# Weight loads issued by ScalarE on their own queue in a two-layer hybrid recurrent decoder

## The chip, the core and the metric

The kernel runs on one core of a Trainium2 chip. A core has a matmul engine (TensorE, PE in the profile, with its weight loads as PEld), three engines for elementwise work (VectorE or DVE, ScalarE or ACT, GpSimd or POOL) and SyncE (SP), which computes nothing and here issues transfers. Each engine takes its own instructions in order; they meet through semaphores. The metric is the device time of one execution in microseconds. Lower is better.

## The reference

One inference step of two layers, in float32, for a prompt of 1024 tokens and for 8 sample sequences of one token each, with the same weights; 1032 token columns in all, model width 1024.

```python
# layer 0
xn = rms(x); proj = xn @ w_in0                      # 1024 x 4632, 24 of the columns are gates
conv_act = silu(causal_conv(conv_in))               # 2560 channels, width 4
y  = group_rms((ssd_scan(...) + d * xs) * silu(z))  # Mamba-2, 16 heads, chunks of 128
hm = (group_rms(mlstm_scan(q, k, v, ...)) + skip * xm) * sigmoid(o)   # 4 heads
x += concat([y, hm]) @ w_out0
x += (silu(rms(x) @ w_gate) * (rms(x) @ w_up)) @ w_down               # hidden 2816
# layer 1
xx = shift(rms(x)) - rms(x)                         # six mixtures xr, xw, xk, xv, xa, xg
r, k, v = xr @ wr, xk @ wk, xv @ wv                 # and low-rank w, a, g
S_t = S_{t-1} diag(w_t) + (S_{t-1} (-kk_t)) (kk_t a_t)^T + v_t k_t^T  # RWKV-7, 16 heads
x += ((group_norm(S_t r_t) + bonus) * g) @ wo
x += swiglu(rms(x))
y = rms(x)
```

All new recurrent states are returned too.

## The kernel before

Activations lie transposed: 128 features on the partitions, token columns along the free dimension, so a matrix product is a loop over tiles of 128 output features, each the sum over 8 tiles of 128 inputs. Float32 products are made of three passes. Every operand is cast to a coarser float32 form (`hi`) and the remainder (`lo`) is kept; `mm3` sums lo times hi, hi times lo and hi times hi.

Weights are therefore read, and then prepared, one output tile at a time, in `wload`: a transfer of 128 x 1024 numbers (512 KB) into a tile `raw`, of which the pool `wraw` has two buffers; then, for each half, ScalarE casts to `whi` (`S.copy`, L175) and VectorE subtracts to get `wlo` (`tt`, through the helper's L145). The pool `whl` has four buffers of 512 columns for `whi` and four for `wlo`. A raw buffer is free for the next weight as soon as VectorE has read its last half. Three places load weights: `wload` (L169), `wdown` in the feed-forward, which reads a row tile of the down projection (L968), and `lora2` in the RWKV projections (L1084). The names in the profile follow the tiles: `raw_g`, `raw_u`, `rawd` (feed-forward gate, up, down), `raw_rw` (RWKV r, k, v), `raw_o` (output gate and output projection of layer 0), `raw_wo`, `raw_in`, `raw_z`, `raw_gate`, and `rawl2w`, `rawl2a`.

All transfers are issued by SyncE, through `dma = SY.dma_start`: these weight loads, the inputs, and the many intermediate tensors that go through scratch memory (`scr_...`), among them the small blocks that the RWKV scan exchanges (`scr_ablk`, `X`, `scr_tblk`, `obd`, `scr_toff`, `tbd`, `vbd`) and the projections' results (`rst`, stored by L1119 from a ring of two buffers).

Work runs in this order, in time of the profiled execution. Until about 850 us: the norm, the input projection with the convolutions, the SSD and mLSTM chunks, the gates' tiles and the output projection for the first half of the tokens. From 850 to 1230: the feed-forward of layer 0 for the first half, with the second half's output projection between. From 1230 to 2000: RWKV projections of the first half, then the scan of the first half (`rwkv_scan`, generators `rw_pre`, `rw_inv`, `rw_front`, `rw_fin`, `rw_ln`) woven into the feed-forward of the second half. From 2000 to 3000: projections of the second half, its scan, the decode steps and the first feed-forward of layer 1. From 3000 on: the last output projection and feed-forward, with no scan beside it.

The order within each engine is not written by hand. The program's text gives each instruction a priority (its place, shifted ahead by `ahead()` for a few), the framework plans the instructions against a model of their times, and places all semaphore waits. Each engine's list, the issues on it included, then runs in that fixed order. So when the issuing engine of a transfer changes, the plan is made anew.

Of the kernel before, what the change touches and what calls it, by code (L numbers as in the profile page):

```python
# [90 lines left out]
def _body(tc, nc, I, O, top):  # L91
    def pool(stack, name, bufs=1, **kw):
        if kw.get("space") is not DRAM:
            kw["reuse_waits"] = "tile"
        return stack.enter_context(tc.tile_pool(name=name, bufs=bufs, **kw))
# [15 lines left out]

    V, S, G, PE, SY = nc.vector, nc.scalar, nc.gpsimd, nc.tensor, nc.sync
    dma = SY.dma_start

    consts = cp.tile([128, NLATE], F32, name="consts")
    dma(out=consts, in_=I["consts"][:, 0:NLATE])
# [27 lines left out]
    def tt(out, a, b, op=ALU.mult, e=None):  # L144
        (e or V).tensor_tensor(out=out, in0=a, in1=b, op=op)  # L145

    def stt(out, a, s, b, op0=ALU.mult, op1=ALU.mult, e=None):
        (e or V).scalar_tensor_tensor(out=out, in0=a, scalar=s, in1=b, op0=op0, op1=op1)  # L148
# [4 lines left out]
    def act(out, a, f, **kw):  # L153
        S.activation(out, a, f, **kw)  # L154
# [11 lines left out]
    def wload(src, name, n=1024, step=128, e=None, th=TA_, p=128):  # L166

        raw = th.wraw.tile([128, 1024], F32, name="raw_" + name, tag="raw")
        dma(out=raw[0:p, 0:n], in_=src)  # L169
        out = []  # L170
        for c0 in range(0, n, 512):
            m = min(512, n - c0)
            hi = th.whl.tile([128, 512], F32R, name=f"whi_{name}{c0}", tag="whi")
            lo = th.whl.tile([128, 512], F32R, name=f"wlo_{name}{c0}", tag="wlo")
            S.copy(hi[0:p, 0:m], raw[0:p, c0:c0 + m])  # L175
            tt(lo[0:p, 0:m], raw[0:p, c0:c0 + m], hi[0:p, 0:m], ALU.subtract, e)
            for q in range(0, m, step):
                out.append((hi[0:p, q:q + step], lo[0:p, q:q + step]))
        return out
# [44 lines left out]
    def ahead():  # L224

        return tc.high_priority(offset=AHEAD)

    def norm_split(src, gname, tp, hl, blocks, base, bank=dbank):
        def emit(k, n0, n, x, g, rs):
            t = tp.tile([128, blocks[-1][1]], F32, name="n_t", tag="nq", bufs=2)  # L230
            stt(t[:, :n], x, g, rs)
            c = slice(n0 - base, n0 - base + n)
            split(t[:, :n], hl[k][0][:, c], hl[k][1][:, c])
        norm(src, gname, tp, emit, blocks, bank)
# [610 lines left out]
    def hl_ring(name, w):  # L845
        return [[H_.hl.tile([128, 520], F32R, name=f"{name}{q}{k}", tag="h" + q)[:, 0:w] for q in "hl"]
                for k in range(8)]
# [77 lines left out]
    def wide(name):  # L925
        return H_.nt.tile([128, 520], F32, name=name, tag="nt", bufs=2)

    def ffn(layer, hf, xs, hook=None, bank=dbank, start=None, ap=None, wide_=lambda f: True):
        base, W = HALF[hf]
        blocks, dblk = HBLK[hf], DBLK[hf]  # L930
        with ExitStack() as st:
            tp = H_.nt
            defer = ap is not None
            ap = ap or pool(st, f"ffna{layer}{hf}", GRP + 1)
            hl = hl_ring(f"f{layer}{hf}", W)
            with ahead():
                norm_split(lambda k, n0, n: xs[k][:, n0 - base:n0 - base + n], f"g_ffn{layer}", tp, hl, blocks, base, bank)
            if start:
                start()

            def up(f, part=False):
                nm = f"{layer}{hf}_{f}"
                wg = wload(I["wgu"][layer, f, 0], "g" + nm)
                wu = wload(I["wgu"][layer, f, 1], "u" + nm)
                ah = ap.tile([128, 520], F32R, name="ah" + nm, tag="ah")
                al = ap.tile([128, 520], F32R, name="al" + nm, tag="al")
                sg = wide("sg" + nm)

                def evg(n0, n, ps):
                    s = sg[:, n0 - base:n0 - base + n]  # L950
                    act(s, ps, AF.Tanh, scale=0.5)
                    stt(s, s, 1.0, ps, ALU.add, ALU.mult)

                def evu(n0, n, ps):
                    c = slice(n0 - base, n0 - base + n)
                    stt(sg[:, c], sg[:, c], 0.5, ps)
                    split(sg[:, c], ah[:, c], al[:, c])
                def tiles(bl):
                    dense_tile(wg, hl, "g" + nm, evg, blocks=bl, base=base)
                    dense_tile(wu, hl, "u" + nm, evu, blocks=bl, base=base)  # L960
                if part:
                    return (ah, al), tiles
                tiles(dblk if f and wide_(f) else blocks)
                return ah, al

            def wdown(f):
                raw = TA_.wraw.tile([128, 1024], F32, name=f"rawd{layer}{hf}{f}", tag="raw")
                dma(out=raw, in_=I["wdn"][layer, f])  # L968
                hi = ap.tile([128, 1024], F32R, name=f"dhi{layer}{hf}{f}", tag="dhi", bufs=GRP)
                lo = ap.tile([128, 1024], F32R, name=f"dlo{layer}{hf}{f}", tag="dlo", bufs=GRP)  # L970
                S.copy(hi, raw)  # L971
                tt(lo[:, 0:512], raw[:, 0:512], hi[:, 0:512], ALU.subtract)
                tt(lo[:, 512:], raw[:, 512:], hi[:, 512:], ALU.subtract)
                return hi, lo

            def down(f, acts, wds, bls=None):
                ev = resid(xs, base)
                for bl in bls or [dblk if wide_(f) else blocks]:
                    for m in range(8):
                        dense_tile([(w[0][:, m * 128:m * 128 + 128], w[1][:, m * 128:m * 128 + 128]) for w in wds],  # L980
                                   acts, f"d{layer}{hf}{f}_{m}", ev(m), blocks=bl, base=base)

            acts = {}
            split_ = hf == 1 and not defer
            for f in range(NFF - split_):
                acts[f] = up(f)
                if hook:
                    hook(f)
                if f % GRP == 0 and f:
                    g = range(f - GRP, f)  # L990
                    down(f, [acts[i] for i in g], wds)
                if f % GRP == GRP - 1:
                    wds = [wdown(i) for i in range(f - GRP + 1, f + 1)]
            if split_:

                acts[NFF - 1], tiles = up(NFF - 1, True)
                hook(NFF - 1)
                wds = [wdown(i) for i in range(NFF - GRP, NFF)]
                for q in blocks:
                    tiles([q])  # L1000
                    down(NFF, [acts[i] for i in range(NFF - GRP, NFF)], wds, [[q]])
            last = lambda bls: down(NFF, [acts[i] for i in range(NFF - GRP, NFF)], wds, bls)
            if defer:
                return lambda: last([[q] for q in blocks])
            if split_:
                return
            last([[q] for q in blocks])
# [13 lines left out]
    def rwkv_proj(hf, xs, xe, hook=lambda c, j: None, vt=None):  # L1021
        base, W = HALF[hf]
        blocks, dblk = HBLK[hf], DBLK[hf]
        with ExitStack() as st:
# [51 lines left out]
            def lora2(i, nm, bias, dst):  # L1076

                w = []

                def tile_(j):  # L1080
                    if j % 4 == 0:

                        raw = TA_.wraw.tile([128, 1024], F32, name=f"rawl2{nm}{hf}{j}", tag="raw")
                        dma(out=raw[:, 0:512], in_=I["wl2"][i, :, j * 128:j * 128 + 512])  # L1084
                        w[:] = [TA_.whl.tile([128, 512], F32R, name=f"l2{nm}{hf}{j}", tag="whi")]
                        S.copy(w[0], raw[:, 0:512])
                        tt(w[0][64:128], raw[64:128, 0:512], w[0][64:128], ALU.subtract)
                    o = j % 4 * 128
                    t = wide("l2t")
                    for n0, n in dblk:  # L1090
                        ps = dbank("l2ps")
                        c = slice(n0 - base, n0 - base + n)
                        PE.matmul(out=ps[:, 0:n], lhsT=w[0][:, o:o + 128], rhs=LH[i][0][:, c], start=True, stop=False)
                        PE.matmul(out=ps[:, 0:n], lhsT=w[0][:, o:o + 128], rhs=LH[i][1][:, c], start=False, stop=True)
                        act(t[:, c], ps[:, 0:n], AF.Tanh, bias=hw0[:, bias + j:bias + j + 1], scale=0.5)
                    dma(out=dst[:, j, base:base + W], in_=t[:, 0:W])
                return tile_
# [768 lines left out]
```

## Time and profile before

| | |
|---|---|
| median of 3 runs | 3487.57 us (3483.46 to 3492.62) |
| profiled execution | 3490.3 us, its span 3488.5 us |
| mean granted TensorE clock | 0.971 |
| TensorE busy | 3233.9 us, 93% |
| VectorE / ScalarE / GpSimd busy | 2329.8 / 1656.6 / 1228.5 us |
| DMA | 458.26 MB in 399135 packets, 43.6% of 16 engines' time on one hardware queue (q1) |

The span goes from the first to the last instruction. Busy shares are averages over stages with different limits, so a stage is read by itself: the rows of stages give start and end, length, and then the busy time and count of PE, PEld, DVE, ACT and POOL, the granted clock, the DMA share and GB/s. The chain is followed back from the last instruction through whatever released each step. A row of the waits says who waited, for whom, the total in us, how many times and the longest. SPq is SyncE's queue; a row of its timeline gives the start and the time that the issue itself took. Rows of one line's instructions give minimum, median and maximum in ns. In rows of groups stand the busy total and mean ns, then the idle time ahead.

### The profile page before, as it was taken

The page shows a single profiled execution, that of the slowest core. Times are in us where ns is not written, and L with a number is a line of the kernel's source. Part 1 is how long each engine was busy: PE and PEld are TensorE (multiplying, and loading weights), DVE is VectorE, ACT ScalarE, POOL GpSimd, SP SyncE. Part 2 cuts the span into 40 slices and gives each one's busy share as a digit, 9 for nine tenths or more (in the row PEclk, how much of TensorE's full clock was granted, in tenths as well). Part 3 has the DMA queues.
Part 4 walks back from the last instruction along what each step waited for, and adds up shares of the span by engine and source line. Part 5 has one row for each costly group of instructions (what it writes and reads, how often), then busy time and mean ns, then how long its engine had stood idle before and what let it go on. Part 6 is the DMA issues. An engine that isn't in the chain of part 4 may idle for free.

```text
span 3488.5 us, 61294 instructions
## 1 busy us (share of the span) xinstructions
PE 3233.9 (93%) x22615; PEld 2990.8 (86%) x22615; DVE 2329.8 (67%) x4315; ACT 1656.6 (47%) x3705; POOL 1228.5 (35%) x1586
## 2 busy tenths in 40 slices
PE   6999978998999999989999978988999899999998
PEld 6998877877778887779999968987888889999998
DVE  8866534566765477676776686667777775575555
ACT  5444344534243245655455565665555554452223
POOL 3334254121200002255645576237767873000000
PEclk9999998999999999999999989999999999999999
DMA  3456586663663343543333323462433333333232
GB/s 118 128 185 201 178 220 178 191 192 124 222 202 109 97 145 110 187 149 98 103 103 102 94 81 122 139 208 74 116 102 103 99 89 116 120 97 99 87 101 67
DMA packets 399135, 458.26 MB, mean 131 GB/s; under 512 B 154756, under 2 KB 295524, under 8 KB 398708
## 3 DMA queue, kind: packets, MB, share of 16 engines
q1 hardware_dynamic: 398836, 454.34, 43.6%
q8 instruction: 179, 2.93, 0.4%
q14 instruction: 120, 0.98, 0.1%
HBM read 352.10 MB, written 102.07 MB: 130 GB/s over the span
## 4 chain that ended last, share of the span: by engine, by line
PE 43%; DVE 13%; POOL 10%; DMA 8%; ACT 5%; issue 4%; SPq 1%; DVEq 0%; ACTq 0%; POOLq 0%
PE ps_g L186 9%; PE ps_d L186 9%; PE ps_u L186 9%; POOL X L145 4%; POOL t L145 4%; PE ps_rw L186 4%; PE ps_out L186 2%; ACT L154 2%; PE ps_o L186 2%; PE ps_wo L186 1%; DVE lp L148 1%; DMA phm<-scr_hmt 1%; DMA raw_rw<-in_wrw 1%; PE M L1403 1%; POOL y L145 1%
## 5 line engine op out<-in xcount | busy, mean ns | idle before, releaser
L186 PE MATMUL ps_d<-al,dhi 128*128 128x260 f32 (+2 forms) x1248 | 386.8, 310 | 20.3 <-DVE xa L145 5.0
L186 PE MATMUL ps_d<-ah,dlo 128*128 128x260 f32 (+2 forms) x1248 | 373.2, 299 | 0.0
L186 PE MATMUL ps_d<-ah,dhi 128*128 128x260 f32 (+2 forms) x1248 | 372.9, 299 | 0.0
L145 POOL TENSOR_TENSOR X<-X,t 32x30 f32<-32x30 f32 (+14 forms) x480 | 307.0, 640 | 32.6
L145 POOL TENSOR_TENSOR t<-X 32x30 f32<-32x30 f32 (+14 forms) x480 | 294.2, 613 | 30.9
L186 PEld LDWEIGHTS ps_d<-al,dhi 128*128 128x128 f32 x1248 | 237.2, 190 | 40.9 <-DVE xa L145 10.5
L186 PEld LDWEIGHTS ps_d<-ah,dlo 128*128 128x128 f32 x1248 | 237.4, 190 | 7.5
L186 PEld LDWEIGHTS ps_d<-ah,dhi 128*128 128x128 f32 x1248 | 236.9, 190 | 7.6 <-issue 0.2
L145 DVE TENSOR_TENSOR wlo_g<-raw_g,whi_g 128x512 fp32r<-128x512 f32 (+1 forms) x192 | 144.5, 755 | 106.1 <-ACT whi_g L175 104.2
L971 ACT CAST dhi<-rawd 128x1024 fp32r<-128x1024 f32 x88 | 88.4, 1046 | 216.6 <-PE ps_d L186 208.9
L154 ACT ACT_TABLE_LOAD x140 | 179.6, 1283 | 8.0 <-DVE ss L145 5.6
L175 ACT CAST whi_g<-raw_g 128x512 fp32r<-128x512 f32 (+1 forms) x192 | 113.9, 599 | 143.0 <-DMA raw_g<-in_wgu 83.3
L145 DVE TENSOR_TENSOR wlo_u<-raw_u,whi_u 128x512 fp32r<-128x512 f32 x176 | 133.9, 761 | 69.1 <-ACT whi_u L175 68.1
L175 ACT CAST whi_u<-raw_u 128x512 fp32r<-128x512 f32 x176 | 107.9, 619 | 134.7 <-PE ps_u L186 100.9
L186 PE MATMUL ps_in<-xnl,whi_in 128*128 128x344 f32 x480 | 155.5, 324 | 1.5 <-ACT ext L289 1.5
L186 PE MATMUL ps_in<-xnh,wlo_in 128*128 128x344 f32 x480 | 155.8, 325 | 0.0
L186 PE MATMUL ps_in<-xnh,whi_in 128*128 128x344 f32 x480 | 154.8, 322 | 0.0
L145 DVE TENSOR_TENSOR dlo<-rawd,dhi 128x512 fp32r<-128x512 f32 x176 | 124.4, 759 | 15.2 <-ACT dhi L971 15.1
L145 POOL TENSOR_TENSOR xx<-xa 128x512 f32<-128x512 f32 x8 | 9.7, 1242 | 346.5 <-PE ps_out L186 346.5
L157 ACT CAST ah<-sg 128x260 fp32r<-128x260 f32 (+2 forms) x155 | 67.5, 435 | 132.0 <-DVE sg L148 130.0
L145 DVE TENSOR_TENSOR wlo_rw<-raw_rw,whi_rw 128x512 fp32r<-128x512 f32 x96 | 72.1, 758 | 80.4 <-ACT whi_rw L175 76.8
L145 POOL TENSOR_TENSOR Bb<-Bc,consts 128x256 f32<-128x256 f32 x64 | 50.8, 793 | 210.3 <-PE M L1403 138.3
(959 smaller groups left out, 11934.7 us busy)
## 6 DMA issues: line engine op xcount, KB each, us to landing
raw_g<-in_wgu SPq DMA_DIRECT2D x88, 512.0 KB
raw_u<-in_wgu SPq DMA_DIRECT2D x88, 512.0 KB
rawd<-in_wdn SPq DMA_DIRECT2D x88, 512.0 KB
raw_rw<-in_wrw SPq DMA_DIRECT2D x48, 512.0 KB
raw_o<-in_wout SPq DMA_DIRECT2D x32, 512.0 KB
raw_in<-in_win SPq DMA_DIRECT2D x20, 512.0 KB
D<-scr_acr SPq DMA_DIRECT2D x16, 512.0 KB
Cs<-in_mc SPq DMA_DIRECT2D x16, 512.0 KB
```

Source lines behind the costliest of these rows:

```text
L145: (e or V).tensor_tensor(out=out, in0=a, in1=b, op=op)
L148: (e or V).scalar_tensor_tensor(out=out, in0=a, scalar=s, in1=b, op0=op0, op1=op1)
L154: S.activation(out, a, f, **kw)
L157: S.copy(hi, src)
L175: S.copy(hi[0:p, 0:m], raw[0:p, c0:c0 + m])
L186: PE.matmul(out=ps, lhsT=w[a], rhs=x[b], start=i == 0, stop=i == n - 1)
L971: S.copy(hi, raw)
L1403: PE.matmul(out=b[:, o + q * 128:o + q * 128 + 128], lhsT=lhs(q), rhs=rhs(q), start=True, stop=True)
```

## The change

A second name, `wdma`, is bound to ScalarE's `dma_start`, and the three places that load weights use it. All other transfers stay on SyncE. Buffers, sizes, casts and the number of transfers stay as they are.

```diff
     V, S, G, PE, SY = nc.vector, nc.scalar, nc.gpsimd, nc.tensor, nc.sync
     dma = SY.dma_start
+    wdma = S.dma_start
...
     def wload(src, name, n=1024, step=128, e=None, th=TA_, p=128):
         raw = th.wraw.tile([128, 1024], F32, name="raw_" + name, tag="raw")
-        dma(out=raw[0:p, 0:n], in_=src)
+        wdma(out=raw[0:p, 0:n], in_=src)
...
             def wdown(f):
                 raw = TA_.wraw.tile([128, 1024], F32, name=f"rawd{layer}{hf}{f}", tag="raw")
-                dma(out=raw, in_=I["wdn"][layer, f])
+                wdma(out=raw, in_=I["wdn"][layer, f])
...
                         raw = TA_.wraw.tile([128, 1024], F32, name=f"rawl2{nm}{hf}{j}", tag="raw")
-                        dma(out=raw[:, 0:512], in_=I["wl2"][i, :, j * 128:j * 128 + 512])
+                        wdma(out=raw[:, 0:512], in_=I["wl2"][i, :, j * 128:j * 128 + 512])
```

## The prediction, made before the change was run

> **What bounds the kernel now.** I read the page first, then the busy time by stage, then the waits of the DMA queue, then single stretches.
>
> ```profile
> span 3488.5 us, 61294 instructions
> PE 3233.9 (93%) x22615; PEld 2990.8 (86%) x22615; DVE 2329.8 (67%) x4315; ACT 1656.6 (47%) x3705; POOL 1228.5 (35%) x1586
> PE 43%; DVE 13%; POOL 10%; DMA 8%; ACT 5%; issue 4%; SPq 1%; DVEq 0%; ACTq 0%; POOLq 0%
> ```
> ```profile
> 0.00:850.00 850.00, 770.73 (x4561) 700.12 (x4562) 534.79 (x863) 389.11 (x928) 271.17 (x238) 0.96 0.57 170
> 850.00:1230.00 380.00, 372.13 (x1825) 298.36 (x1824) 230.87 (x385) 123.99 (x196) 29.25 (x24) 0.99 0.49 160
> 1230.00:2000.00 770.00, 734.75 (x5247) 678.95 (x5245) 547.17 (x1027) 407.44 (x877) 333.04 (x465) 0.99 0.42 123
> 2000.00:3000.00 1000.00, 886.65 (x7109) 847.57 (x7108) 723.86 (x1405) 566.15 (x1385) 595.04 (x860) 0.95 0.40 113
> 3000.00:3110.00 110.00, 107.79 (x879) 105.58 (x878) 75.65 (x174) 56.18 (x110) 0.00 (x0) 1.00 0.29 92
> 3110.00:3488.00 378.00, 361.83 (x3006) 360.27 (x3004) 217.47 (x464) 113.75 (x210) 0.00 (x0) 0.98 0.30 94
> ```
>
> TensorE (first number after the length) is the bound: 93% busy, 255 us idle in all. The feed-forward stretches (850 to 1230, 3000 to 3488) leave it idle 8, 2 and 16 us; nothing that moves DMA issues can matter there. The idle time sits in 0 to 850 (79 us), 1230 to 2000 (35 us) and above all 2000 to 3000 (113 us), where the recurrent scan runs between the projections. There ScalarE (fourth engine number) is busy 566 of 1000 us and VectorE 724. So what the change is worth is decided in the scan and, less, in the opening. On the chain that ended last, DMA has 8% (279 us), ScalarE 5%, the SP queue itself 1% (35 us).
>
> Now the queue from which the weight loads are taken.
>
> ```profile
> SPq L169 <- DVE dlo L145: 293.2, 66, 30.3
> SPq L968 <- DVE wlo_g L145: 148.4, 31, 22.4
> SPq L169 <- DVE wlo_g L145: 109.3, 40, 8.6
> SPq L169 <- DVE wlo_rw L145: 93.9, 35, 13.3
> SPq L169 <- DVE wlo_o L145: 67.5, 23, 10.7
> SPq L169 <- DMA raw_g<-in_wgu: 42.8, 23, 3.3
> SPq L169 <- DMA raw_rw<-in_wrw: 11.8, 8, 2.5
> ```
>
> L169 and L968 are the weight loads. The five VectorE rows alone add up to 712 us, a fifth of the span, in which SP stands at a weight load until VectorE has taken the low part out of the raw buffer (two buffers). The queue keeps order, so whatever lies behind stands too. One such place:
>
> ```profile
> 2163.56 0.33 SPq L169 DMA_DIRECT2D raw_g<-in_wg  x1
> 2172.60 0.33 SPq L169 DMA_DIRECT2D raw_w<-in_wl  x1
> 2173.03 0.38 SPq L1119 DMA_DIRECT2D scr_kr<-rst  x1
> ```
> ```profile
> 2172.16 0.41 DVE L145 TENSOR_TENSOR wlo_g<-raw_g,whi_g 128x256 fp32r<-128x256 f32 x1
> ```
> ```profile
> 2168.97 0.37 ACT L1117 COPY rst<-ps_rw 128x260 f32<-128x260 f32 x1
> 2171.43 1.31 ACT L1063 CAST xc1h<-lp 128x260 fp32r<-128x260 f32 x3
> ```
>
> SP stands from 2163.9 to 2172.6, until VectorE's wlo_g ends at 2172.57. The store scr_kr behind it was ready when ScalarE's copy ended at 2169.34: held 3.7 us by a load that has nothing to do with it. That is what the change removes. But in the same microseconds ScalarE was doing useful casts (1.31 us from 2171.43); with the load in ScalarE's own stream, these could have been what stood.
>
> **The change, part by part.**
>
> *Issue time.* Weight loads per line:
>
> ```profile
> L169 SPq DMA_DIRECT2D raw_g<-in_wgu x88: 327/333/595, 768.7 to 3422.2; - x88
> L169 SPq DMA_DIRECT2D raw_gate<-in_win x1: 401/401/401, 14.4 to 14.4; - x1
> L968 SPq DMA_DIRECT2D rawd<-in_wdn x88: 327/334/577, 822.7 to 3438.1; - x88
> ```
>
> From the first to the last group there are 429 (88 raw_g of in_wgu, 88 raw_u, 88 rawd, 48 raw_rw, 40 raw_o, 20 raw_in, 16 raw_g of in_wg, 16 raw_wo, 25 in smaller groups). At 0.333 us, 143 us of sequencer time leave SP and enter ScalarE, which goes from 47% to 51%. No row shows an issue on ScalarE, so I take SP's; bounds 0 and 0.6 us, the longest in the first row. How much lies on the path: ScalarE has 5% of the chain for 47% of the span, one ninth of its time. 143/9 is **+15 us** (0 to +28). In the feed-forward stretches ScalarE's idle time covers it wholly (114 of 378 us busy in the last).
>
> *The wait moves with the load.* A load waits for the raw buffer's last subtraction on VectorE.
>
> ```profile
> L145 DVE TENSOR_TENSOR wlo_g<-raw_g,whi_g 128x512 fp32r<-128x512 f32 (+1 forms) x192 | 144.5, 755 | 106.1 <-ACT whi_g L175 104.2
> ```
>
> That subtraction takes 0.755 us and starts when ScalarE's cast ends. Behind the waiting load on ScalarE are the next evictions, exponentials and casts; TensorE waits for the evictions through its PSUM banks, VectorE for the casts (the row: 104.2 us of waiting for whi_g already). Low end: the planner puts other ready ScalarE work between cast and load, hold 0. High end: ScalarE stands out one subtraction for each of 429 loads, 324 us, a ninth of it 36 us. The two places I can read differ: at 2172 ScalarE had three casts to lose; in the steady feed-forward it had nothing to do:
>
> ```profile
> 3206.08 2.00 ACT L971 CAST dhi<-rawd 128x1024 fp32r<-128x1024 f32 x2 [10.13 <-PE ps_d L186]
> ```
>
> Ten idle microseconds cover the hold there. Between the two I take the middle, **+18 us** (0 to +36).
>
> The Trainium skill speaks to this point: "Perfetto Trace Analysis", section "DMA Instruction — HWDGE (DVE, Sync)", has the semaphore wait and the descriptor generation on the issuing sequencer, which is free only when both are over. By that rule the hold tends to its high end and the sum to 3521 us; the 8.7 us at 2172 agree for SP, and no row here shows ScalarE doing it.
>
> *Completion counters.* The SP queue also waits for old transfers:
>
> ```profile
> 2221.78 0.35 SPq L1119 DMA_DIRECT2D scr_rt<-rst  x1
> 2222.30 0.82 SPq L1417 DMA_DIRECT2D tbd<-scr_tblk  x2
> 2223.21 0.40 SPq L1096 DMA_DIRECT2D scr_tw<-l2t  x1
> 2223.66 0.47 SPq L1419 DMA_DIRECT2D tbd<-scr_toff  x1
> 2224.18 0.94 SPq L1417 DMA_DIRECT2D tbd<-scr_tblk  x2
> 2225.55 0.30 SPq L1419 DMA_DIRECT2D tbd<-scr_toff  x1
> 2226.33 0.35 SPq L169 DMA_DIRECT2D raw_rw<-in_wrw  x1
> ```
> ```profile
> 2221.78 4.48 DMA scr_rt<-rst
> 2226.33 3.68 DMA raw_rw<-in_wrw
> ```
>
> The chain goes from the store scr_rt (4.48 us) straight into a weight load that uses none of its data; the load is the ninth transfer, counting the store as first. I read this as eight completion counters used in turn. The diff adds none, so I expect ScalarE's loads to take their turn in the same eight and then to wait for a transfer of SP eight back. The two DMA rows of the waits give 54.6 us of it at L169; on ScalarE a ninth is **+6 us** (0 if ScalarE gets its own counters, +55 if all lands on the path, since it ties ScalarE to a queue that may lag).
>
> *What SP gains.* SP loses 143 us of issues and at least 712 us of standing. Its own chain share is 35 us and DMA's 279 us. Low bound 0: most held transfers are prefetches. High bound: the 35 us and a fifth (SP's standing share, 712/3488) of 279, together 91 us. The weight loads themselves gain almost nothing, for SP stood ready at the buffer's release. I take **−22 us**, a quarter, because the chain's large pieces are TensorE and the POOL and VectorE steps of the scan, not held transfers.
>
> *The opening.*
>
> ```profile
> 2.60 11.72 SPq L325 DMA_DIRECT2D xin<-in_xT  x24
> 14.39 0.40 SPq L169 DMA_DIRECT2D raw_gate<-in_win  x1
> ```
> ```profile
> 24.52 0.66 PE L186 MATMUL ps_gate<-xnl,whi_gate 128*128 128x344 f32 x1 [1.53 <-ACT whi_gate L175]
> ```
>
> The first weight load stands behind 24 loads of x; on its own queue it goes out at the start. TensorE waited 1.53 us for its cast: **−1.5 us** (0 to −1.5), and x shares the engines with it, at no visible price.
>
> Sum: 15 + 18 + 6 − 22 − 1.5 = +15.5 on the profiled execution's 3490.3 us (span 3488.5 and 1.8 around it): 3506. The median of the three runs, 3487.57, is 2.7 below that execution, so I forecast **3503 us**, 0.4% slower. The order of every engine is planned anew with the loads on ScalarE; no row prices that, and it widens both sides.
>
> **The rivals.**
>
> *Faster, 3458 us.* The scan's small transfers no longer stand behind weight loads. For it: scr_kr held 3.7 us, 712 us of standing, 113 us of idle TensorE in 2000 to 3000. Against: ScalarE's work is in that same scan. With two thirds of the high bound gained (61 us), the opening, and ScalarE's costs at their low side (issue 15, hold 15, counters 2): 3487.6 − 61 − 1.5 + 32 is 3457. It decides once the gain exceeds the 39 us that ScalarE's three terms cost.
>
> *No change, 3488 us.* ScalarE is idle 53% of the span and the planner can put the issues there; SP was free when it mattered. For it: SPq is 1% of the chain. Then 15 us of issue meet 15 us of gain. The Trainium skill's "DMA: Bandwidth & Descriptors", section "Issuing engines are not separate DMA queues", has all issuing engines share the same 16 DMA engines, so that only issue time is saved. By that rule this rival is the likeliest; the 8% of the chain that is transfer time cannot test it in a trace with one queue in use.
>
> *Much slower, 3570 us.* ScalarE follows SP through the counters and through VectorE's late subtractions: hold 36, counters 55, issue 28 and no gain: 3488 + 119 is 3607; with a third of that missing, 3567.
>
> **How the numbers follow.** Slower as forecast 0.34, much slower 0.07, no change 0.28, faster 0.31. The three runs of before lie within 0.13% of their median, so I count 0.3% (10.5 us) as the least that can be told. That gives faster 0.31, within 0.28, slower 0.41. The range 3440 to 3585 reaches past the faster rival by 18 us (all of the 91 us gained would give about 3436) and to most of the much slower one. The forecast's own range is 3498 to 3545.
>
> **What would show it.** Right: a second queue with about 216 MB (the 405 loads of 512 KB among the 429, and the smaller ones); weight loads listed under ScalarE at about 0.33 us; ScalarE's waits with rows that start at L169 or L968, on VectorE's low parts, of 100 us or more; 3110 to 3488 unchanged within 2 us; SP's standing at weight loads gone. Wrong on the sign: TensorE's idle time in 2000 to 3000 falls under 95 us while ScalarE's new waits stay under 50 us. Wrong on the counters: no ScalarE load ever waits for a transfer of SP. The forecast fails as a whole if the planned order of the scan changes so much that its stages no longer answer to these.

## Result, and the profile after

The changed kernel takes 3533.81 us (median of 4 executions, 3530.34 to 3536.04), the kernel before on the same chip 3489.97 (4 executions). The ratio is 1.0133, 95% interval 1.0119 to 1.0148: slower by 44 us. The forecast was 3503 us, 0.4% slower, with a range of 3440 to 3585.

The head of the page of the changed kernel, and its rows of DMA queues (packets, MB, share of 16 engines' time):

```profile
span 3533.9 us, 61023 instructions
PE 3249.2 (92%) x22615; PEld 3004.7 (85%) x22615; DVE 2322.6 (66%) x4315; ACT 1660.7 (47%) x3705; POOL 1227.1 (35%) x1586
q1 hardware_dynamic: 337060, 237.79, 23.3%
q10 hardware_dynamic: 61776, 216.56, 19.9%
```

The change did what it says: a second queue carries 216.56 MB. The span grew by 45.4 us. Of these, 15.3 are TensorE busy longer with the same 22615 matmuls (its mean granted clock was 0.967, and 0.971 before), and 30.1 are idle time of TensorE (254.6 before, 284.7 after). The longer busy time fits the new idle time: the clock record of the trace has TensorE at full or at half clock, and the half-clock stretches (most of them 3.4 or 6.8 us long) grow from 32 with 207 us to 39 with 235 us. In the 3.4 us ahead of such a stretch TensorE stands idle for 2.4 us in the mean, against 0.2 to 0.3 us over the whole kernel, in both traces.

The same stages, by the changed kernel's windows. The first four are cut at the times of before, the last one is moved by the 45 us by which the kernel is late there:

```profile
0.00:850.00 850.00, 767.45 (x4556) 698.53 (x4557) 533.83 (x865) 390.73 (x928) 275.09 (x238) 0.97 0.57 170
850.00:1230.00 380.00, 370.43 (x1802) 296.12 (x1801) 226.91 (x381) 122.91 (x194) 29.47 (x24) 0.99 0.49 159
1230.00:2000.00 770.00, 724.75 (x5139) 670.67 (x5138) 538.01 (x1007) 402.70 (x856) 328.09 (x462) 0.99 0.42 122
2000.00:3000.00 1000.00, 877.86 (x6938) 835.40 (x6937) 709.12 (x1380) 554.83 (x1372) 590.23 (x859) 0.94 0.38 110
```
```profile
3155.00:3533.00 378.00, 360.80 (x3000) 359.38 (x2998) 214.85 (x455) 110.58 (x207) 0.00 (x0) 0.98 0.29 92
```

In the same windows TensorE does 3 us less work in the opening, 2 less in the feed-forward, 10 less from 1230 to 2000 and 9 less from 2000 to 3000; the scan stage also ends later now. The last feed-forward is as before (360.80 busy, 361.83 before). To see where the delay arises I matched each ScalarE instruction with the same one of the other profile; the medians by start time in before are:

```
start in before, us      50-100  200-250  450-500  800-850  1100-1150  1500-1550  1950-2000  2350-2400  2700-2750  2950-3000  after 3000
later in after, us          5.1      9.6      8.1      0.8        3.8        9.5       14.0       28.3       32.8       37.0  43 to 45
```

The opening's loss is absorbed by 800 us. From there to the end the kernel loses 44 us, two thirds of them from 1950 on, where the scan of the second half runs; the last feed-forward adds nothing.

### The profile page after: what moved, and what is told of

Read it like the earlier page. It is cut to its first block, busy times and chain, and to the rows that moved or that the text cites. A ratio compares the mean times of both kernels' runs of the same rounds, so it can differ in the third digit from the quotient of the medians.

```text
span 3533.9 us, 61023 instructions
## 1 busy us (share of the span) xinstructions
PE 3249.2 (92%) x22615; PEld 3004.7 (85%) x22615; DVE 2322.6 (66%) x4315; ACT 1660.7 (47%) x3705; POOL 1227.1 (35%) x1586
## 3 DMA queue, kind: packets, MB, share of 16 engines
q10 hardware_dynamic: 61776, 216.56, 19.9%
q8 instruction: 179, 2.93, 0.4%
```

## Experiments

The comparisons ran on four occasions; before measured 3491.8, 3491.5, 3483.8 and, for the last run, 3493.9 us. Each ratio is to the kernel before on the same chip. The theories: **hold** (H in the first expectations: ScalarE stands for the raw buffer's release), **issue** (I: its own time for 429 issues), **sharing** (Q: weights on a queue of their own make the scan's small transfers land later), **order** (P: the plan is made anew, and the new one is worse).

### Hold on ScalarE without its loads: touch

```diff
+        S.copy(raw[:, 0:1], eps)
         dma(out=raw[0:p, 0:n], in_=src)
```
(at all three places; loads stay with SyncE)

> All loads stay on SyncE, in one queue. Before each weight load ScalarE writes one column of its raw buffer, so ScalarE waits for the buffer at the place where the changed kernel issues the load, and the load waits for ScalarE. Theory H (ScalarE stands at the weight loads until VectorE frees the buffer, and its following work is late): most of the 44 us come back without a second queue, 3510 to 3540 us. Rival Q (the second queue shares the 16 DMA engines and makes the scan's small transfers land later): at most 3497 us, the price of 429 ScalarE operations of about 0.2 us, a ninth of them on the path. Rival I (issue time of 0.334 us on ScalarE): as Q, 3497 us.

Measured: 3503.9 us, ratio 1.0040 (1.0027 to 1.0053). In the groups of the trace, the added writes have a busy total, a mean, the idle time ahead of them and whom they waited for:

```profile
L169 ACT COPY raw_g<-eps 128x1 f32<-128x1 f32 x104 | 19.8, 190 | 68.4 <-DVE wlo_g L145 34.9 <-DVE dlo L145 26.4 <-DVE wlo_wo L145 2.8
L969 ACT COPY rawd<-eps 128x1 f32<-128x1 f32 x88 | 16.8, 191 | 59.4 <-DVE wlo_g L145 42.2 <-DVE wlo_u L145 14.4 <-DVE dlo L145 2.3
L169 ACT COPY raw_u<-eps 128x1 f32<-128x1 f32 x88 | 16.7, 190 | 36.9 <-DVE dlo L145 24.0 <-DVE wlo_u L145 9.2 <-DVE wlo_wo L145 1.6
```

All groups of these writes together stand 239 us. In the changed kernel, matching each ScalarE load with the release of its buffer gives some 250 us of standing. So touch has the change's hold nearly whole, and 82 us of added work, and costs some 14 us with all else that it brings (784 ScalarE instructions stand elsewhere, too). The time lies between the bands, above the 3497 us of Q and I and below the 3510 of H: the hold alone does not bring back the 44 us.

### Added ScalarE time without hold: op1

The same copy of one column into a buffer of its own, so that it waits for nothing:

```diff
+        S.copy(junk, eps)
         dma(out=raw[0:p, 0:n], in_=src)
```

> The kernel before with one added ScalarE copy of one column (0.19 us, like the one that writes into the raw buffer in touch) per weight load, here into a buffer of its own, so that it never waits for VectorE. Touch measured 3503.9 against 3491.8. If touch's 12 us are the hold at the raw buffer, this kernel is within 4 us of before (3488 to 3496). If they are the added ScalarE time (429 x 0.19 = 82 us, a ninth of it 9 us), it comes out at 3499 to 3506, and the hold of some 240 us that touch shows costs nearly nothing. The sharing theory says nothing of this run.

Measured: 3495.48 us, ratio 1.0008 (0.9997 to 1.0018). 82 us of ScalarE work spread over the kernel can't be told from nothing, and the upper end, 0.18% or 6.3 us, stays under the ninth of it, 9 us. By the expectation that leaves touch's 12 us to the hold; but touch has a new order and op1 has not, so the order is a rival for them. This run kept the order of before: 22 of TensorE's 22615 instructions stand elsewhere.

### A new plan, first try: pert1

One unused copy on ScalarE at the start, to make the framework plan anew:

```diff
     V.memset(eps, EPS)
+    S.copy(eps2, eps)
```

> The kernel before with one more ScalarE copy of one column at the start, 0.2 us of work that nobody uses: it measures what a new plan of all engines does by itself. H, Q and I: within 5 us of the kernel before. Rival P (any new plan moves the time by tens of us, and the change drew a bad one): off by more than 10 us, to either side.

Measured: 3491.64 us, ratio 1.0002 (0.9991 to 1.0013). By its time alone this looks like a plan that costs nothing. But the orders of the two traces are the same: not one instruction of any compute engine has moved. The run says nothing about the order.

### An issue per load with hardly a byte: tiny, tread, tdram

Three attempts to have ScalarE issue 429 small transfers while the weights stay with SyncE. In tiny:

```diff
+        S.copy(t, hi)                                   # one column of raw
+        S.dma_start(out=TINY[tn[0]].unsqueeze(1), in_=t)  # 128 x 4 bytes
```

> All weight loads stay on SyncE. For each of them ScalarE copies one column of the raw buffer to a small tile (eight of them) and issues a 512 byte store of it: 429 issues on ScalarE's queue that take their turn in the completion counters, but wait for no VectorE result. H: 3490 to 3505 us. I: 3515 to 3535 us. Completion counters as the cause: 3515 us or more. Q: little, since the second queue carries almost no bytes, at most 3497 us.

Measured: 5338.1 us, ratio 1.5296 (1.5275 to 1.5317). All expectations missed.

```profile
q1 hardware_dynamic: 398836, 454.34, 57.0%
q10 hardware_dynamic: 61776, 0.25, 0.7%
```
```profile
ACT tiny L121 <- DMA rawd<-in_wdn: 590.5, 71, 14.3
```

The second queue moved a quarter of a megabyte and took 0.7% of the engines' time, and yet the weights' transfers landed 9.61 us after their issue (median; 3.77 before); the last row is ScalarE's copy waiting for them. SyncE's issues also stood 258 us, at 71 places, until one of the small stores had landed and given its completion counter free. The 429 stores of 128 times 4 bytes held up so much that the issue's price can't be read here.

In tread the small transfer is a read of 16 rows of 512 bytes into one of two spare buffers, behind touch's write:

```diff
+        S.copy(raw[:, 0:1], eps)
+        S.dma_start(out=t, in_=src[0:16, 0:128])      # t: 16 x 128, two buffers
```

> Touch (loads on SyncE, ScalarE first writes one column of the raw buffer and so stands until VectorE has released it), and behind each such write ScalarE issues a small load of 16 x 512 B into a buffer that nothing reads: the hold, the issue time and the turn in the shared completion counters of the change, but 3.5 MB on the second queue in place of 216.6. Hold, issue and counters together as the cause: 3520 to 3536 (touch 3504 plus 429 issues of 0.3 us, a ninth of them 14 us, or more). Sharing of the DMA engines by the weights as the cause: 3503 to 3512, and X<-ablk lands at 2.5 to 2.7 us mean as before; the rest up to 3534 needs the weights' bytes on the second queue.

Measured: 3635.3 us, ratio 1.0407 (1.0392 to 1.0422), above every expectation. The two buffers made ScalarE wait for its own reads, in the longest such rows:

```profile
ACT ext L297 <- DMA dump<-in_wgu: 35.7, 14, 5.1
ACT th L163 <- DMA dump<-in_wrw: 21.3, 3, 8.8
```

All such rows on ScalarE add up to 240 us, and the time rose by 131 us over touch, where 239 us at VectorE's release had come with some 14. Tread also runs in an order of its own (907 of 3564 ScalarE instructions moved), so this is no price of standing for a transfer.

In tdram the 16 rows go to a place in memory of their own, so that nothing is waited for:

```diff
+        S.copy(raw[:, 0:1], eps)
+        S.dma_start(out=DUMP[dn[0]], in_=src[0:16, 0:128])
```

> The run tread mended: its two dump buffers made ScalarE wait for its own reads. Here, behind each write into the raw buffer, ScalarE issues a copy of 16 x 512 B from the weights to a place in memory of its own, so that nothing is waited for; the weight loads stay with SyncE. ScalarE has the hold, an issue per load and the turn in the shared counters, and the second queue carries 3.5 MB in place of 216.6. Hold, issue and counters as the cause of the 44 us: 3520 to 3536. The weights' bytes on the second queue as the cause of what touch (3504) leaves open: 3503 to 3512, with X<-ablk at 2.5 to 2.75 us mean.

Measured: 3503.61 us, ratio 1.0059 (1.0046 to 1.0072). The time itself lies in the band of sharing, but before was 8 us faster on that chip: 20 us slower, half of the change. X<-ablk landed after 2.42 us (mean). Hold, issue and the turn in the counters together don't make the change's 1.0133, though an issue took ScalarE 0.58 us here and 0.334 in the change. Since tdram also runs in a new order of its own (937 of 3564 ScalarE instructions moved), even 1.0059 is no price of these three alone.

### Part of the loads: ffnonly, projonly

Only the 264 feed-forward loads on ScalarE, and only the other 165:

```diff
-        wdma(out=raw[0:p, 0:n], in_=src)
+        (wdma if ffn_ else dma)(out=raw[0:p, 0:n], in_=src)      # ffnonly
+        (dma if ffn_ else wdma)(out=raw[0:p, 0:n], in_=src)      # projonly
```
(against the changed kernel; `ffn_` is true for the feed-forward's gate and up weights; wdown and the lora loads accordingly)

> Only the feed-forward's 264 loads (gate, up, down) go through ScalarE; the other 165 stay on SyncE. H: the 264 loads cost where the feed-forward runs beside the scan (1500 to 2000 and 2400 to 3000), nothing in the pure feed-forward; the delay had grown by about 24 us in those two stretches, so 3505 to 3520 us. P: anywhere within 20 us of 3490.

Measured: 3512.9 us, ratio 1.0058 (1.0045 to 1.0071), in the band of H and 3 us above that of P.

> Only the 165 weight loads that are not the feed-forward's go out on ScalarE; the 264 of the feed-forward stay with SyncE. The feed-forward's alone cost 21 us (3512.9 against 3491.8), all 429 cost 44 us. If the parts add up (hold or issue time, both per load), this kernel takes 3510 to 3519. If the scan's small transfers landing later behind the feed-forward's weights is what costs, this half costs less: 3495 to 3505, and X<-ablk lands at 2.7 us mean or below (2.60 before, 3.07 with the feed-forward's loads on ScalarE, 3.49 with all).

Measured: 3509.38 us, ratio 1.0046 (1.0033 to 1.0060), 18 us, between the two bands; X<-ablk at 2.93 us, above its bound for sharing. The two parts cost 21 and 18 us, about what the whole costs. That fits any cause that comes per load, and did not tell the theories apart; both also run in new orders (644 and 661 ScalarE instructions moved).

### Weights on GpSimd: pool

```diff
-    wdma = S.dma_start
+    wdma = G.dma_start
```
(against the changed kernel)

> All 429 weight loads on GpSimd: a queue apart from SyncE's, as in the change, but nothing of it in ScalarE's stream. Sharing of the DMA engines by two queues as the cause: X<-ablk lands at 3.3 us mean or later as in the change (before 2.60), and the time is 3515 or more even where GpSimd's own standing is short. ScalarE's stream as the cause: X<-ablk at 2.5 to 2.8 us, and the time follows GpSimd's standing in the scan, where it is busy 595 of 1000 us: 3490 to 3600. In both, GpSimd stands for VectorE's low parts by 100 us or more.

Measured: 3548.06 us, ratio 1.0177 (1.0159 to 1.0195). Two queues again, but X<-ablk lands after 2.79 us, not 3.3, so a second queue alone does not bring the late landing. (GpSimd's queue is listed as software_dynamic, ScalarE's as hardware_dynamic, so the two need not act alike.) The loads in GpSimd's list:

```profile
L969 POOL DMA_DIRECT2D rawd<-in_wdn x88 | 49.3, 560 | 296.3 <-DVE wlo_g L146 160.5 <-DVE wlo_u L146 109.7 <-DVE xb L146 7.1
L170 POOL DMA_DIRECT2D raw_g<-in_wgu x88 | 49.1, 558 | 409.9 <-DVE dlo L146 232.1 <-DVE wlo_g L146 97.9 <-DMA raw_u<-in_wgu 30.9
```

GpSimd stood 706 us ahead of these two groups; an issue took it 0.56 us, where ScalarE takes 0.334. The order moved more than in the change, too (1033 ScalarE instructions).

### Others taken off SyncE's queue: stores, xpool

Weights stay with SyncE; in stores, what ScalarE has just computed is stored by ScalarE, in xpool X is loaded and stored by GpSimd, which computes on it:

```diff
+    adma = S.dma_start
...
-            dma(out=dst[:, i, :], in_=sg)
+            adma(out=dst[:, i, :], in_=sg)               # stores: here and in six more places
...
-        dma(out=X, in_=ABLK[hf, j])
+        G.dma_start(out=X, in_=ABLK[hf, j])              # xpool
...
-        dma(out=TBLK[hf, j], in_=X)
+        G.dma_start(out=TBLK[hf, j], in_=X)
```

> Weight loads stay with SyncE; the stores of what ScalarE itself has computed last (the projections' results and the gates', some 200 stores) go out from ScalarE, so that they no longer stand behind a weight load that waits for its raw buffer, and ScalarE waits for nothing that it hasn't just done itself. If standing behind weight loads costs the scan anything, this is faster than before: 3465 to 3485. If the held transfers are hidden, as the change's missing gain suggests, 3488 to 3496; with issue time counting in full (200 x 0.33, a ninth of it 7 us) up to 3500.

Measured: 3497.35 us, ratio 1.0017 (1.0008 to 1.0027).

> Weight loads stay with SyncE; only the load of the inversion's blocks X and the store of its result (16 of each) go out from GpSimd, which computes on X. In the kernel before, X's load is issued 4.5 us (mean; median 2.2) after the stores that it reads have landed, since SyncE stands elsewhere, and GpSimd waits 62 us for it in all. If that standing sets the end, the time falls by up to the 62 us: 3450 to 3480. If it is covered by other work, 3486 to 3497. If loads apart from the weights' queue land later (sharing), X lands at 3 us or more, not 2.60.

Measured: 3493.94 us, ratio 1.0028 (1.0014 to 1.0042), in the band for covered work, though before was 3483.8 on that chip.

```profile
POOL X L1357 <- DMA X<-scr_ablk: 43.1, 16, 4.6
POOL X L1356 <- DMA scr_ablk<-As: 37.4, 12, 8.3
```

GpSimd's wait for X fell from 62 us to 43, but 37 came up at the issue itself, for the stores that X reads. Neither kernel gains time by taking transfers out from behind the weight loads. Both also run in new orders (518 and 471 ScalarE instructions moved), so a gain that the order ate up is not excluded. X landed after 3.27 us (mean), as the sharing theory has it, and the time hardly moved.

### The order alone: planonly

The traces had shown that the changed kernel runs 2856 of TensorE's 22615 instructions, 987 of VectorE's and 751 of ScalarE's out of before's sequence. The last run takes the kernel before and pins every engine's list, weight loads aside, to the order of the changed kernel:

```diff
         body(tc, I, O)
+        pin(tc, nc)      # each instruction behind its predecessor in the written-down order:
+                         # issue order only, no wait for its end
```

> The kernel before, weight loads on SyncE's queue, but every engine's instructions, and SyncE's other transfers, are pinned to the order in which the changed kernel has them (the weight loads alone are free). ScalarE has no load, no hold and no issue; one queue carries everything. What is left of the change is its new order of the work: 2856 of TensorE's 22615 instructions, 987 of VectorE's 4315 and 751 of ScalarE's 3564 stand elsewhere than before. If the order costs nothing: ratio to before 0.997 to 1.003. If it is what tdram (1.0059 of before) leaves of the change's 1.0133: 1.005 to 1.009. If it is all of it, and hold and issue are covered: 1.011 to 1.015. Weights' bytes on the second queue as the cause of the rest: the first of the three, with X<-ablk landing at 2.4 to 2.8 us mean.

Measured: 3538.43 us, ratio 1.0128 (1.0106 to 1.0150): the third band, as slow as the change itself, with every transfer on SyncE's queue and nothing of it on ScalarE. The pin held: by the two traces no instruction of the compute engines, and no transfer but weight loads, stands elsewhere than in the changed kernel. X<-ablk landed after 2.80 us (mean).

```profile
span 3543.7 us, 61288 instructions
PE 3253.5 (92%) x22615; PEld 3010.1 (85%) x22615; DVE 2333.4 (66%) x4315; ACT 1655.9 (47%) x3705; POOL 1231.5 (35%) x1586
```

TensorE's busy time is up as in the change (19.6 us over before, the change 15.3), at a granted clock of 0.964 and with 39 half-clock stretches as in the change, and its idle time is 290.2 us. SyncE stands at the weight loads as it did before:

```profile
SPq L169 <- DVE dlo L145: 293.2, 68, 30.3
SPq L968 <- DVE wlo_g L145: 133.8, 27, 22.1
```

The same waits of TensorE, in before, in the changed kernel and in planonly:

```profile
PE n_ps L212 <- DVE n_acc L145: 20.7, 5, 7.9
PE fin L1463 <- DVE y L1478: 12.2, 8, 4.1
PE ps_g1a L186 <- DVE xc1l L145: 1.7, 1, 1.7
PE kks L164 <- POOL sql L145: 2.1, 3, 1.1
```
```profile
PE n_ps L213 <- DVE n_acc L146: 42.2, 6, 17.0
PE fin L1464 <- DVE y L1479: 23.8, 9, 6.6
PE ps_g1a L187 <- DVE xc1l L146: 7.9, 3, 4.6
PE kks L165 <- POOL sql L146: 7.3, 2, 4.5
```
```profile
PE n_ps L212 <- DVE n_acc L145: 55.3, 5, 29.7
PE fin L1463 <- DVE y L1478: 22.2, 11, 6.7
PE ps_g1a L186 <- DVE xc1l L145: 8.2, 4, 4.7
PE kks L164 <- POOL sql L145: 7.5, 2, 4.6
```

In the last three rows the changed kernel and planonly agree to a microsecond or two, down to the longest single wait, and before stands apart. These are places where the order makes TensorE wait, whichever queue brings the weights. They do not stand alone: of TensorE's waits outside n_ps (by what waits and for what), the change moved 25 by more than 2 us, up or down, and 22 of these moved the same way in planonly.

The first row is a flaw of planonly. In the changed order ScalarE casts whi_gate ahead of the norm, which needs an early weight; on SyncE's queue that weight stands behind the 24 loads of x. In planonly's timeline:

```profile
15.15 0.40 SPq L169 DMA_DIRECT2D raw_gate<-in_win  x1
20.31 1.14 ACT L175 CAST whi_gate<-raw_gate 128x512 fp32r<-128x512 f32 x2 [18.29 <-DMA raw_gate<-in_win]
29.75 1.52 PE L212 MATMUL n_ps<-n_acc,consts 128*128 128x344 f32 x2 [29.75 <-DVE n_acc L145]
```

TensorE's first matmul comes at 29.75 us in place of 12.05 in before, so some 17.7 us of planonly's loss are its own. Taken off the whole 44.6 us of the medians, that leaves 27. By the matched instructions of the profiled executions (planonly's is 7 us above its median), planonly loses 35.1 us between 800 us and the end (20.1 to 55.2), the changed kernel 44.4 (0.8 to 45.2). Up to 1950 to 2000 the two lose much the same, 11 and 13 us; from there on 24 and 31. So the order accounts for about 27 to 35 of the 44 us. The rest, some 9 to 17, is what moving the loads costs in one and the same order: hold, issue, counters and sharing together, less what SyncE gains.

## Why the prediction was right and wrong

The direction was right and the range held, but the sum reached the 44 us only to a third, and the largest cost is not among its terms. That the measured time lies in the range is luck as far as the mechanism goes: it is owed to the width of the range, not to the sum. What the sum does price, hold, issue and counters less SyncE's gain, +17 without the opening, is not contradicted by the 9 to 17 us left at equal order; but the runs don't split these into its terms, and sharing, which it left out, is among them.

*Order: named, not priced.* The prediction said that "the order of every engine is planned anew with the loads on ScalarE; no row prices that". This is the step that failed: the widening should have been a term, of some 27 to 35 us. The prediction's last sign, a planned order so changed that the scan's stages no longer answer to its signs, names the same thing: the stages can still be read, but most of the loss is in the order. Across the runs, the two whose order stayed have ratios of 1.0002 and 1.0008; the ten whose order changed are all slower, the mildest 1.0017. These ten carry other costs too, and tiny and tread are of no use here, but planonly shows that order by itself can make 1.0128 (some of it the flaw above). How much moves does not set the price: tdram moved 3561 of TensorE's instructions, more than the change, for 1.0059.

*Issue time, +15.* ScalarE's issues are as short as SyncE's:

```profile
L170 ACTq DMA_DIRECT2D raw_g<-in_wgu x88: 334/334/377, 769.9 to 3467.5; - x88
```

The 143 us are right (a ninth of them is 15.9, not 15). The ninth on the path is not shown: 82 us of added work in op1 cost 0.08%, the interval includes zero, and its upper end, 6.3 us for 82, would make 11 us of the 143. This is an estimate from op1, whose added work was copies, not issues.

*The wait moves with the load, +18.* The mechanism is there:

```profile
ACT whi_u L176 <- DVE wlo_g L146: 11.3, 5, 4.8
ACT sg L155 <- DVE dlo L146: 10.1, 3, 8.4
ACT av L1429 <- DVE wlo_g L146: 6.1, 1, 6.1
```

Such rows make 70.9 us in all, none before, where the prediction's sign was 100 us or more; but they show only loads behind which ScalarE had something ready. By the releases it stood some 250 us, three quarters of the 324 of the high end. "Perfetto Trace Analysis" of the Trainium skill, section "DMA Instruction — HWDGE (DVE, Sync)", has the wait sit on the issuing sequencer; the trace agrees, with an 8.07 us wait (the last of the three durations in the row below, in ns) on ScalarE's own sequencer at L170. But standing is not time: touch, with 239 us of it, cost some 14 us (1.0040, upper end 1.0053).

```profile
L170 ACTq EVENT_SEMAPHORE  x216: 17/17/8067, 9.7 to 3461.8; - x108
```

*Completion counters, +6.* Right in kind: the eight counters are used in turn by both queues, and a few of ScalarE's loads waited, some 9 us in all, for the counter's last transfer. The other direction, which the prediction did not price, is larger: SyncE's issues stood 23.0 us, at 15 places, until one of ScalarE's weight loads had landed. What either is worth in time is not shown.

*SP's gain, −22.* Not shown. SyncE no longer stands at weight loads, but stores and xpool, which take transfers out from behind them from the other side, gained nothing either (in new orders of their own). SyncE now stands at the next thing:

```profile
SPq L1120 <- ACT rst L1118: 179.0, 42, 37.0
SPq L1418 <- PE Z L1404: 119.2, 25, 12.5
```

Dropping this term alone would have given 3525 us, nearer, and for a reason that the runs don't show.

*The opening, −1.5.* Wrong in sign. The early weights did go out at 0.75 us, and x paid for it (a load of x landed after up to 6.8 us, before after 4.2 at most), in the changed kernel's timeline:

```profile
2.83 17.87 SPq L326 DMA_DIRECT2D xin<-in_xT  x24
17.05 1.51 PE L213 MATMUL n_ps<-n_acc,consts 128*128 128x344 f32 x2 [17.05 <-DVE n_acc L146]
```

The 24 issues of x stretch from 11.72 us to 17.87, and TensorE's first matmul comes 5.0 us later (17.05 us, before 12.05). The third of these issues waited 1.5 us for the counter of a weight load, and ScalarE now casts whi_gate and whi_in ahead of the norm. "At no visible price" was the misreading: before had one queue, so nothing could show the price. By 800 us this loss was made up.

*The faster rival* did not occur. *No change* is borne out by op1 as to added ScalarE work; that the held transfers are covered fits stores and xpool and is not shown. The Trainium skill's "DMA: Bandwidth & Descriptors", section "Issuing engines are not separate DMA queues", would have had only issue time saved; the time got worse instead, for a reason outside that rule. *Much slower* through hold and counters did not occur.

*What the runs leave open.* Which of the moved instructions cost the time is not shown; the three waits above are places, and their growth of some 23 us in the changed kernel is no proof that it is the path's. Nor are the last 9 to 17 us split between hold, issue, counters and sharing. An order planned for two queues may also fit one queue badly, beyond the opening: planonly can't exclude that, though the rows above grow with two queues as well. The opposite test, loads on ScalarE in the order of before, was not tried. Nor was a third raw buffer.

## What to carry to other kernels

Where a framework plans the order, moving an instruction to another engine is two changes: the move, and a new plan. Compare the two orders before explaining a difference by waits, and pin one kernel to the other's order to split the two; a control that is meant to disturb the plan must be seen to have moved something. The time that an engine stands says little of what the kernel loses: 239 us on ScalarE, idle half the time, came with some 14 here, and 712 us of SyncE ahead of prefetches went without a gain that shows.

## What the hardware showed unexpectedly

A queue that moves almost nothing can slow another: with 429 stores of 128 times 4 bytes each on ScalarE's queue the kernel was 1.53 times as long, and tbd<-tblk landed after 5.24 us (mean; 2.13 before), though X<-ablk hardly moved (2.66 us, 2.60 before). With the weights on ScalarE's queue the scan's small loads land later (X<-ablk 3.49 us in the mean of 16, 2.60 before and 2.80 in planonly, in the same order; tbd, obd and vbd move less, obd to 2.65 from 2.43), while the weights themselves land as before (3.75 us median, 3.77 before). And the same TensorE work took 15 to 20 us longer at a granted clock lower by 0.004 to 0.007, with no matmul changed: 39 half-clock stretches in place of 32, nearly all behind idle time of TensorE.
